# Low parts of seven weight tiles made by a ScalarE cast and an adding transfer instead of a VectorE subtraction

## The chip, the cores and the metric

The program runs on one core of one Trainium2 chip. The metric is the device time of one execution in microseconds (us), here the median of three runs. The profile is that of one further execution. Engines: PE is TensorE (PEld its weight loads), DVE is VectorE, ACT is ScalarE, POOL is GpSimd, SP is SyncE, which here only issues transfers.

## The reference, cut to what matters

Two transformer layers run over 256 context and 256 latent tokens of width 1024. The first layer mixes tokens by an mLSTM, the second by latent attention, and each is followed by a gated feed-forward with a convolution over time:

```python
def _conv_ffn(h, w_in, conv_w, conv_b, w_out):
    gate, up = jnp.split(h @ w_in, 2, axis=-1)
    return (jax.nn.silu(_dwconv(gate, conv_w, conv_b)) * up) @ w_out
...
x = _layer_norm(ALPHA * x + ml[2] * yl, ln_g[i, 0], ln_b[i, 0])
f = _conv_ffn(_modulate(x, ml[3], ml[4]), ffn_w_in[i], ffn_conv_w[i], ffn_conv_b[i], ffn_w_out[i])
x = _layer_norm(ALPHA * x + ml[5] * f, ln_g[i, 1], ln_b[i, 1])
```

The change is in the product `h @ w_in` of the second layer's feed-forward. There only the 256 latent tokens are left, and `w_in` is 1024 x 5632: 22 blocks of 128 columns of the gate and 22 of the up half.

## The kernel before, in words

**Products in two parts.** Every fp32 matrix is used as a sum of a rounded high part and a low part, both in the type fp32r, and a product is three matmuls: high by high, high by low, low by high. For weights the two parts are made on the fly by the class `Stream`. One tile is 128 x 1024 fp32 (512 KB). SP loads it into a raw buffer (`_load`, L308), ACT casts it to the high part h (`_split`, L345), and DVE writes the low part l = raw - h (`low`, L368). When the low part is made the raw buffer is given back (`self.raw.pop(j)`), and the next load may be issued into it. The order of all weight tiles is one list, made by `_plan`.

**Where the parts live.** A tile that is not `wide` takes one of NB = 3 buffers `w` that hold both parts. A `wide` tile takes two of the 31 general buffers `u` instead, which also hold activations, and is not counted against the three. `Stream.use(key)` hands out the next tile, and first calls `_split` for later tiles, up to AHEAD = 8 tiles past it, as long as the next one is wide or fewer than three `w` tiles are alive. From the attention output weights on, raw buffers are taken in a ring of nine: three of their own, three `u`, and three freed by other work.

**Order.** The program is written engine by engine as dataflow. A planner orders the instructions of each engine once, before the run, by the order of the program text and by its own estimate of when operands are ready, so an instruction may be put ahead of others that were written earlier. At run time each engine and each queue works through its list in order; waits are semaphores.

**The stage.** `aout_fin` ends the attention, normalizes, and starts the second feed-forward's input with its first five tiles: (`fin1`, p, j) for block p = 0, 1 and half j = 0, 1 (wide), and (2, 0). `ffn_in(1, ...)` takes the other 39 tiles in the order (2, 1), (3, 0), (3, 1), ... (21, 1). For one tile `both_mm` (L1503) issues 16 matmuls: eight of the high weights with 512 columns (the high and low parts of the 256 tokens side by side) and eight of the low weights with 256 columns, in the order seven high, eight low, one high. Then ACT copies half of the PSUM result (L1620) and DVE adds the halves (L1621). For each block the convolution, SiLU and gating follow (L728 to L735 on ACT and DVE, L1640), and the result is split into the tile `act` (L1648 ACT, L1649 DVE).

**Around it.** Through the first tiles of the stage a background generator, `ln_x`, finishes the residual: eight 512-column operations on DVE (L1518, L1520), each pair followed by a store that POOL issues (L1521, `x3d`). From about 1256 us on POOL issues the loads of the last normalization (L1566, L1215). After the stage, `outmm` multiplies the 22 `act` tiles by `w_out` (tiles `fout1`, matmul lines L430, L433, L434, results `y`), and `ln_rows` (L1229 on) ends the program on DVE and ACT.

Transfers that add to their destination exist already: for eight tiles of an earlier product, SP loads a first matrix, then POOL issues a transfer that adds a second one from device memory (L306), into a raw buffer of plain fp32. None of the kernel's transfers of that kind has its source in on-chip memory.

Of the kernel before, what the change touches and what calls it, by code (L numbers as in the profile page):

```python
# [11 lines left out]
ALU = mybir.AluOpType  # L12
# [58 lines left out]

YTAIL = 3


def _stat(w, m, kt0, nkt):
    k = w.shape[0] // 128
    a = w.reshape(k, 128, w.shape[1])[kt0:kt0 + nkt, :, m * 128:(m + 1) * 128]
    return a.transpose(1, 0, 2).reshape(128, nkt * 128)
# [7 lines left out]
def _plan():  # L86
    ids, order = {}, []

    def add(key, cols, wide=False):
        if key not in ids:  # L90
            ids[key] = (len(ids), cols)
        order.append((key, wide))

    for m in range(NUP, 16):
        add(("up", m, 0), 1024)
    for s in range(4):
        for c in range(4):
            add(("og", s, c), 1024)
    for p in range(2):

        for j in range(4):
            for n in ("vt2", "v11", "vt3", "vt1"):
                add((n, p, j), 1024)
        for j in range(4):
            for n in ("v21", "vt4", "v22"):
                add((n, p, j), 1024)
    for h in range(H0):
        for j in range(4):
            for c in range(2):
                add(("qk", (h * 2 + j) if j < 2 else (8 + h * 2 + j - 2), c), 1024)  # L110
    for g in range(2):
        for k in range(16):
            add(("mout", 0, k), 1024, k in MWIDE if g == 0 else k >= 16 - WIDE["mout"])
    for p in range(NF):
        add(("fin0", p, 0), 1024)
        add(("fin0", p, 1), 1024)
    cols = [1024] * 5 + [512]
    for j in range(6):
        for n in ("yt2", "y11", "yt3", "yt1"):
            add((n, 0, j), cols[j])  # L120
    for n in ("y21", "y22", "yt4"):
        for j in range(6):
            if (n, j) == ("yt4", 6 - YTAIL):
                for c, m in enumerate((3, 3, 2)):
                    add(("dkv", 0, c), m * 320)
            add((n, 0, j), cols[j], n == "yt4" and j >= 6 - YTAIL)
    for c in range(2):
        add(("ukn", 0, c), 1024, True)
    for c in range(2):
        add(("uv", 0, c), 1024, True)  # L130
    for c in range(4):
        add(("dq", 0, c), 768)
    for c, n in enumerate((2, 1)):
        add(("uqr", 0, c), n * 512)
    for c in range(3):
        add(("uqn", 0, c), 1024)
    for k in range(8):
        add(("aout", 0, k), 1024, k >= 8 - WIDE["aout"])
    for p in range(NF):
        add(("fin1", p, 0), 1024, p < 2)  # L140
        add(("fin1", p, 1), 1024, p < 2)
    for k in range(NF):
        add(("fout1", 0, k), 1024, k >= NF - WIDE["fout1"])
    return ids, order


def _pack(i):
    ids, _ = _plan()
    ws = np.zeros((len(ids), 128, CW), np.float32)
    gz = np.concatenate([i["m_w_gates"][0, 0], i["m_w_gates"][0, 1]], axis=1)  # L150
# [107 lines left out]
class Stream:  # L258
# [105 lines left out]
        return self.k.pool.tile([128, CW], F32R, tag="u", name="wu", bufs=NU)  # L364

    def low(self, j, src, h, l):
        n = src.shape[1]
        i = self.k.nc.vector.tensor_sub(l[:, :n], src, h[:, :n])  # L368
        self.k.behind(i, self.behind)
        self.made = i  # L370
        if self.order[j][0] == ("y21", 0, 1):
            self.second = i
        self.raw.pop(j)
        while self._room():
            self._load()
        return i
# [24 lines left out]
class K:  # L401
# [933 lines left out]
    def aout_fin(self, o1, pl, xr, gate, fi, h1u, att):  # L1335
# [21 lines left out]
        st.later = []  # L1357
        st.pump(fi + 4)
        low, st.later = st.later, None
        st.behind = lastw  # L1360
        st.pump(fi + 5)
# [570 lines left out]
    def ukn(self, g, heads=range(H1), held=None):  # L1932

        cs = slice(g * 256, (g + 1) * 256)
        for h in heads:
            w = self.wk[h // 4]
            if h % 2 == 0:
                ps = self.ps("kn")
            hs = slice((h % 2) * 256, (h % 2 + 1) * 256)
            for k in range(2):  # L1940
                c = slice((h % 4) * 256 + k * 128, (h % 4) * 256 + (k + 1) * 128)
                self.mm3(ps[:, hs], (w[0][:, c], w[1][:, c]), (self.ckT[k][:, 0, cs], self.ckT[k][:, 1, cs]),
                         k == 0, k == 1)
            if h % 2:
                lows = []
                for j in range(2):
                    hi, lo, src = self.kn[h - 1 + j][:, 0, cs], self.kn[h - 1 + j][:, 1, cs], ps[:, j * 256:(j + 1) * 256]
                    i = self.nc.scalar.copy(hi, src)
                    if held is not None:
                        self.tc.keep_in_program_order(i)  # L1950
                    lows.append(lambda lo=lo, src=src, hi=hi: self.nc.vector.tensor_sub(lo, src, hi))
                if held is not None:
                    held += lows
                else:
                    for low in lows:
                        low()
# [225 lines left out]
def build(tc, off, a, out):  # L2182
    es = ExitStack()
    with es:
        k = K(tc, es, off, a)
        nc = k.nc
        ids, order = _plan()
        k.st = st = Stream(k, ids, order, a["ws"])
        k.setup()
# [117 lines left out]
        for low in held:  # L2307
            k.behind(low(), k.normed)
# [54 lines left out]
```

## Time and profile before

| | |
|---|---|
| Runs | 1347.71, 1347.18, 1347.31 us; median 1347.31 |
| Profiled execution | span 1345.3 us from first to last instruction; 2.0 us less than the median of the runs, which also hold what lies before and after the span |
| Granted TensorE clock | 0.998 mean over the span, 1.00 in the changed stage |
| Busy share | PE 99%, PEld 83%, DVE 79%, ACT 53%, POOL 11% |
| Second feed-forward's input | matmuls from 1151.9 to 1276.3 us; the 39 tiles of `ffn_in` from 1167.35 us |
| Second feed-forward's output | 1276.3 to 1337.5 us, then 7.7 us of normalization and store |

Busy shares are means over the whole span; what an edit in one stage can move is read from that stage's rows. In a timeline row the first number is the start in us after the span's first instruction, the second the duration in us; brackets give the engine's idle time just before the row and what ended it.

### The profile page before, as it was taken

The numbers are of one execution on the slowest core, as the hardware profiler recorded it, in microseconds if no ns is written. First come the engines' busy times: TensorE is split into PE (matmuls) and PEld (weight loads), VectorE is DVE, ScalarE is ACT, GpSimd is POOL, SyncE is SP. The second block draws the span as 40 slices with busy tenths as digits, with TensorE's granted clock in tenths as the row PEclk, the third lists the DMA queues.
The fourth block names the chain that finished last, engine by engine and source line by source line (L and its number), as shares of the span: only waits on it lengthen the run. The fifth ranks groups of instructions, "written<-read, shape, count | busy, mean of one in ns | idle before, by whom it ended". The sixth has DMA issues, their size and how long they took to land.

```text
span 1345.3 us, 18750 instructions
## 1 busy us (share of the span) xinstructions
PE 1334.9 (99%) x6659; PEld 1120.2 (83%) x6659; DVE 1059.0 (79%) x1745; ACT 711.7 (53%) x1252; POOL 141.5 (11%) x236
## 2 busy tenths in 40 slices
PE   9999999999999999999999999999999999999997
PEld 5777888888888888888898888888888998988886
DVE  4798656678688696897979977758899889898874
ACT  4765444445744546474644334333566767676660
POOL 0222000011101011020002011111000002000100
PEclk9999999999999999999999999999999999999999
DMA  9988848889686384776628989967866437376750
GB/s 364 330 277 279 281 163 248 233 272 307 235 281 230 102 255 149 228 292 222 215 86 261 328 260 286 282 181 184 300 223 194 157 104 219 127 212 189 263 189 32
DMA packets 99885, 304.02 MB, mean 226 GB/s; under 512 B 12312, under 2 KB 25112, under 8 KB 99712
## 3 DMA queue, kind: packets, MB, share of 16 engines
q1 hardware_dynamic: 62992, 218.65, 48.6%
q0 software_dynamic: 26000, 66.75, 17.9%
q10 hardware_dynamic: 10800, 17.44, 3.6%
q8 instruction: 52, 0.85, 0.3%
q14 instruction: 41, 0.34, 0.1%
HBM read 272.21 MB, written 42.12 MB: 234 GB/s over the span
## 4 chain that ended last, share of the span: by engine, by line
PE 97%; DMA 1%; DVE 1%; ACT 0%; issue 0%; SPq 0%; DVEq 0%; ACTq 0%
PE fin L1503 8%; PE tok L430 6%; PE tok L434 6%; PE tok L433 6%; PE fin L433 6%; PE fin L434 6%; PE y L433 6%; PE fin L430 6%; PE y L434 6%; PE y L430 6%; PE qk L430 4%; PE qk L433 4%; PE qk L434 4%; PE up L718 2%; PE up L430 2%; PE up L434 1%
## 5 line engine op out<-in xcount | busy, mean ns | idle before, releaser
L368 DVE TENSOR_TENSOR w<-raw,w 128x1024 fp32r<-128x1024 f32 (+2 forms) x286 | 343.2, 1203 | 131.9 <-ACT w L345 129.7
L345 ACT CAST w<-raw 128x1024 fp32r<-128x1024 f32 (+2 forms) x286 | 296.2, 1037 | 282.4 <-PE tok L434 77.8
L544 DVE SCALAR_TENSOR_TENSOR junk<-ar,bc 128x1024 f32<-128x1024 f32 x128 | 156.1, 1219 | 5.2 <-ACT bc L586 2.3
L433 PE MATMUL fin<-h,w 128*128 128x512 f32 (+1 forms) x370 | 139.6, 377 | 0.0
L430 PE MATMUL fin<-h,w 128*128 128x512 f32 (+1 forms) x370 | 139.5, 377 | 0.0
L434 PE MATMUL fin<-h,w 128*128 128x512 f32 (+1 forms) x370 | 139.3, 377 | 0.0
L1503 PE MATMUL fin<-h,w 128*128 128x512 f32 (+1 forms) x636 | 111.1, 337 | 0.0
L1503 PEld LDWEIGHTS fin<-h,w 128*128 128x128 f32 x636 | 97.6, 190 | 13.2
L430 PE MATMUL qk<-xc,w 128*128 128x512 f32 x256 | 100.2, 391 | 0.0
L434 PE MATMUL qk<-xc,w 128*128 128x512 f32 x256 | 99.8, 390 | 0.0
L433 PE MATMUL qk<-xc,w 128*128 128x512 f32 x256 | 99.6, 389 | 0.0
L433 PEld LDWEIGHTS fin<-h,w 128*128 128x128 f32 x370 | 69.6, 188 | 13.0
L430 PEld LDWEIGHTS fin<-h,w 128*128 128x128 f32 x370 | 69.6, 188 | 12.9
L434 PEld LDWEIGHTS fin<-h,w 128*128 128x128 f32 x370 | 69.6, 188 | 12.6
L434 PEld LDWEIGHTS qk<-xc,w 128*128 128x128 f32 x256 | 48.0, 188 | 10.1
L430 PEld LDWEIGHTS qk<-xc,w 128*128 128x128 f32 x256 | 48.1, 188 | 9.8
L433 PEld LDWEIGHTS qk<-xc,w 128*128 128x128 f32 x256 | 48.1, 188 | 9.8
L430 PE MATMUL tok<-w,hT 128*128 128x512 f32 x128 | 49.9, 390 | 0.0
L433 PE MATMUL tok<-w,hT 128*128 128x512 f32 x128 | 49.8, 389 | 0.0
L434 PE MATMUL tok<-w,hT 128*128 128x512 f32 x128 | 49.8, 389 | 0.0
L735 ACT ACTIVATE fg<-fg 128x512 f32<-128x512 f32 (+1 forms) x44 | 23.1, 525 | 50.0 <-DVE fg L733 43.9
L368 DVE TENSOR_TENSOR wu<-raw,wu 128x1024 fp32r<-128x1024 f32 (+1 forms) x37 | 43.8, 1203 | 3.5 <-ACT wu L345 3.2
(486 smaller groups left out, 3125.7 us busy)
## 6 DMA issues: line engine op xcount, KB each, us to landing
raw<-in_ws SPq DMA_DIRECT2D x282, 512.0 KB, 4.5
ar<-in_adaT SPq DMA_DIRECT2D x80, 512.0 KB, 6.0
t4d<-in_ws POOLq DMA_DIRECT2D x20, 512.0 KB, 9.1
adaw<-in_ada SPq DMA_DIRECT2D x16, 512.0 KB, 8.0
zr<-fd ACTq DMA_DIRECT2D x33, 128.0 KB, 4.6
xmd<-xr POOLq DMA_DIRECT2D x16, 256.0 KB, 4.4
xcd<-cv POOLq DMA_DIRECT2D x16, 256.0 KB, 4.9
xs<-xmd POOLq DMA_DIRECT2D x16, 256.0 KB, 6.0
```

What stands on the lines that cost most here:

```text
L345: self.cast = k.nc.scalar.copy(h[:, :cols], src)
L368: i = self.k.nc.vector.tensor_sub(l[:, :n], src, h[:, :n])
L430: q = mm(out, w[0], x[0], start=start, stop=False, skip_group_check=on)
L433: mm(out, w[0], x[1], start=False, stop=False, skip_group_check=on)
L434: mm(out, w[1], x[0], start=False, stop=stop, skip_group_check=on)
L544: nc.vector.scalar_tensor_tensor(o, w, 1.0, self.bc[j], op0=ALU.mult, op1=ALU.mult, accum_out=col[:, k, j:j + 1])
L718: nc.tensor.matmul(ps[m], wk[i][:, c], hT[k][:, j], start=made[m] == 0, stop=made[m] == 23)
L735: nc.scalar.activation(tmp[:, :n], tmp[:, :n], AF.Silu)
L1503: self.nc.tensor.matmul(ps[:, 0:256] if x else ps, w[x][:, k * 128:(k + 1) * 128], h[:, 0:256] if x else h, start=i == 0 and not k0, stop= ...
```

## The change

Seven tiles, the up half (j = 1) of blocks p = 4 to 10, become wide: `_plan` marks them so, and their high and low parts go to two `u` buffers. Their low part is no longer written by DVE. ACT writes l = -raw, rounded to fp32r (the negative of h), and then POOL issues a transfer that adds the raw tile to l, from raw buffer to l buffer, both on chip. The raw buffer is free again when that transfer has landed. All other tiles keep the subtraction on DVE.

```diff
+DLOW = range(4, 11)
...
         add(("fin1", p, 0), 1024, p < 2)
-        add(("fin1", p, 1), 1024, p < 2)
+        add(("fin1", p, 1), 1024, p < 2 or p in DLOW)
...
     def low(self, j, src, h, l):
-        n = src.shape[1]
-        i = self.k.nc.vector.tensor_sub(l[:, :n], src, h[:, :n])
+        n, key = src.shape[1], self.order[j][0]
+        if key[0] == "fin1" and key[1] in DLOW and key[2]:
+            self.k.nc.scalar.mul(l, src, -1.0)
+            i = self.k.nc.gpsimd.dma_start(l, src, accum_op=ALU.add)
+        else:
+            i = self.k.nc.vector.tensor_sub(l[:, :n], src, h[:, :n])
```

## The prediction, made before the change was run

> **What bounds the kernel now.** I read the busy shares first, then the stage in windows, then the matmul row of that stage, because a share of 99% does not yet say whether the matmuls follow each other at their own pace.
>
> ```profile
> PE 1334.9 (99%) x6659; PEld 1120.2 (83%) x6659; DVE 1059.0 (79%) x1745; ACT 711.7 (53%) x1252; POOL 141.5 (11%) x236
> ...
> 1170.00:1200.00 30.00, 30.00 (x172) 26.32 (x171) 28.47 (x54) 22.27 (x43) 1.63 (x3) 1.00 0.62 195
> 1200.00:1260.00 60.00, 60.00 (x347) 52.84 (x346) 51.69 (x86) 40.84 (x77) 1.09 (x2) 1.00 0.65 193
> 1260.00:1280.00 20.00, 20.00 (x115) 17.53 (x114) 17.23 (x29) 14.25 (x26) 4.30 (x8) 1.00 0.92 315
> 1280.00:1320.00 40.00, 40.00 (x216) 34.59 (x215) 22.81 (x20) 19.91 (x21) 0.00 (x0) 1.00 0.44 145
> ```
>
> The columns of a window are its length, then busy time and count of PE, PEld, DVE, ACT and POOL, the granted clock, the busy share of the DMA engines and GB/s. From 1170 to 1320 us PE is busy throughout at clock 1.00. DVE is nearly full only from 1170 to 1200 (28.47 of 30 us); after that it has 8.3 us free in 60. The DMA engines stand at 0.62 to 0.65.
>
> ```profile
> 1167.35 109.10 PE L1503 MATMUL fin<-h,w 128*128 128x512 f32 x624
> 1276.28 0.40 PE L430 MATMUL y<-w,act 128*128 128x512 f32 x1
> 1220.62 0.37 ACT L1620 COPY fs<-fin 128x256 f32<-128x256 f32 x1 [1.17 <-PE fin L1503]
> 1226.20 0.37 ACT L1620 COPY fs<-fin 128x256 f32<-128x256 f32 x1 [1.17 <-PE fin L1503]
> ```
>
> The 624 matmuls are the 39 tiles of the stage, 16 each. They start at 1167.35 and the next stage's first matmul at 1276.28: 108.93 us, 2.793 us a tile. In the undisturbed middle the copy that waits for PE comes every 5.58 us for two tiles, 2.79 us a tile. So all 39 tiles together lose about 39 x 0.003 = 0.1 us to waits. PE is the bound here by its own pace, and a faster low part has 0.1 us to win.
>
> **What is removed.** Seven DVE subtractions.
>
> ```profile
> L368 DVE TENSOR_TENSOR w<-raw,w 128x1024 fp32r<-128x1024 f32 x42 | 51.3, 1223 | 6.3 <-ACT w L345 6.2
> L345 ACT CAST w<-raw 128x1024 fp32r<-128x1024 f32 x41 | 42.9, 1047 | 5.7 <-PE fin L1503 5.4 <-PE y L434 0.3
> L728 ACT ACTIVATE fg<-fs,sm 128x256 f32<-128x256 f32 x22 | 13.2, 600 | 0.5 <-DVE fs L1621 0.4
> L1620 ACT COPY fs<-fin 128x256 f32<-128x256 f32 x44 | 16.3, 370 | 26.9 <-PE fin L1503 25.8 <-PE fin L1489 0.9
> ```
>
> These groups are cut to 1160 to 1280 us. Seven times 1.223 is 8.6 us off DVE. None of it was on the path: worth 0, at most the 0.1 us above.
>
> **What is added on ACT.** Seven multiplications of 128 x 1024. The trace has none of that form; nearest is the cast of the same size, 1.047 us, which I take: 7.3 us. As an upper end, an activation with per-partition operands on 256 columns takes 0.600 against 0.370 for a copy, 0.23 more, so 1.28 us each, 9.0 us; fewer than the seven copies cannot be had, so the lower end is 7.3. ACT is free for 7.7 of the 30 us to 1200 and 19.2 of the next 60. The pressure is in the first 30: four tiles' multiplications (4.2 us) and about three casts that move forward (3.1 us) are 7.3 of 7.7 us. [...] Cost 0.
>
> **What moves: the run-ahead.** Wide tiles do not count against the three `w` buffers, so with every second tile wide, `use` splits five to seven tiles ahead instead of two. Tiles before the seven, and those well after them, keep their old lead. The first wide tile, (4, 1), is cast without waiting for PE to free a `w` buffer. Before, it did wait:
>
> ```profile
> 1163.71 1.05 ACT L345 CAST w<-raw 128x1024 fp32r<-128x1024 f32 x1 [4.54 <-PE fin L1503]
> 1170.95 1.05 ACT L345 CAST w<-raw 128x1024 fp32r<-128x1024 f32 x1
> 1173.14 1.05 ACT L345 CAST w<-raw 128x1024 fp32r<-128x1024 f32 x1 [0.84 <-PE fin L1503]
> 1178.53 1.21 DVE L368 TENSOR_TENSOR w<-raw,w 128x1024 fp32r<-128x1024 f32 x1
> 1181.96 0.37 ACT L1620 COPY fs<-fin 128x256 f32<-128x256 f32 x1 [0.25 <-PE fin L1503]
> ```
>
> The casts are those of tiles (3, 1), (4, 0) and (4, 1) in turn: counting the tiles of `ffn_in` from (2, 1) at 1167.35, the third `w` buffer comes free once per tile. The cast at 1173.14 was released by PE and not by its load, so its raw data lay ready. ACT stood idle for 4.54 us up to 1163.71; the planner puts later work into such holes, for it put the casts of (2, 1) and (3, 0) ahead of a normalization step that is written earlier:
>
> ```profile
> 1139.57 2.01 ACT L345 CAST w<-raw 128x1024 fp32r<-128x1024 f32 x2
> 1143.83 0.29 ACT L1380 ACTIVATE rs<-mv,keps 128x1 f32<-128x1 f32 x1 [2.26 <-DVE mv L1379]
> ```
>
> **What is added on POOL and the DMA engines.** Seven issues and seven 0.5 MB transfers that add. The nearest rows are the eight adding loads from device memory, and POOL's stores in this stage.
>
> ```profile
> L306 POOL DMA_DIRECT2D raw<-in_ws x8: 850/870/903, 218.6 to 324.7; - x8
> ...
> DMA to landing us min/median/max: 6.9/8.6/9.9
> 1168.90 0.55 POOL L1521 DMA_DIRECT2D x3d<-z  x1 [37.13 <-DVE z L1520]
> 1176.09 0.54 POOL L1521 DMA_DIRECT2D x3d<-z  x1 [3.18 <-ACT act L1648]
> 1256.58 0.55 POOL L1566 DMA_DIRECT2D xres<-x3d  x1 [79.94 <-ACT fg L735]
> ```
>
> An issue is 0.55 to 0.87 us, seven are 3.9 to 6.1 us on a POOL that idles from 1176.6 to 1256.6 us. From issue to landing I take 6.9 to 9.9 us, median 8.6. POOL works in order: an adding transfer that waits for ACT holds up the stores of `x3d` written behind it, and these are read back only after 1256 us, so 80 us cover them. The other way round, a store that waits for DVE (the last at 1176.09) holds up an adding transfer behind it; that is in the second case below.
>
> **When the first low part is needed.** PE finished tile (4, 1) just before the copy at 1181.96. Eight low matmuls and the last high one stand at its end; at 2.79 us a tile, the low ones are 0.12 us and the high ones 0.23, so 1.2 us: needed at 1180.8. Best case: cast and multiplication fill the hole before 1163.71, from 1159.2 to 1161.3; issued there, the transfer lands at 1168 to 1171, ten us early. Worst case: cast not before 1173.14, multiplied by 1175.2, landed at 1182.1 to 1185.1, and if queued behind the last store (1176.6) at 1183.5 to 1186.5: 1.3 to 5.7 us late. I take the early case as the likelier, since a raw tile in place, 4.54 idle us and free `u` buffers are what the planner needs. Later wide tiles have five or more tiles of 2.79 us between cast and use, 14 us, against 1.05 + 0.87 + 9.9 = 11.8 us: on time.
>
> [...]
>
> **Waits on PE.**
>
> ```profile
> L1503 PEldq EVENT_SEMAPHORE  x36: 51/51/51, 1172.6 to 1270.4; - x36
> ```
>
> The low weights now wait for a transfer and no longer for DVE. One more wait instruction per tile is 7 x 0.051 = 0.4 us if nothing hides it; the 36 there already, 1.8 us, cost at most the 0.1 us above, so 0.
>
> **Raw buffers and loads.** A raw buffer is now held until the transfer has landed, about 9 us longer for every second tile, and SP's list is in order behind it.
>
> ```profile
> SPq L308 <- DVE fg L1640: 34.6, 11, 3.5
> SPq L308 <- DVE act L1649: 22.0, 10, 2.2
> SPq L308 <- DVE w L368: 2.0, 1, 2.0
> L308 SPq DMA_DIRECT2D raw<-in_ws x54: 327/328/328, 1160.7 to 1301.5; - x54
> ...
> DMA to landing us min/median/max: 3.3/4.0/5.9
> ```
>
> From 1200 to 1260 SP waits 58.6 of 60 us for a buffer, and a load lands in 4.0 us; loads are held by buffers, not by bandwidth. Nine buffers turn once in 9 x 2.79 = 25.1 us. A plain tile needs 4.0 + 1.05 + 1.22 = 6.3 us of it, one of the seven 4.0 + 1.05 + 1.05 + 0.87 + 8.6 = 15.6: on average 14 us to spare. Cost 0.
>
> **Sum.** 0 removed from the path, 0 added: span 1345.3 and, with the 2.0 us around it, the median of 1347.3 again. Its own range is 1346.8 to 1348.0 (0.1 us gain, 0.4 us of waits, and the spread of the runs).
>
> **The rivals.** (A) *The first low part is late*, slower. Place: PE at the low matmuls of (4, 1). It decides if the adding transfer lands after 1180.8. For it: casts of that stretch ran late, POOL's last store issues at 1176.09, and no row tells whether the planner's estimate of an on-chip adding transfer holds. Against: the idle hole and the raw tile in place. Price 1.3 to 5.7 us, middle 3.5: 1350.8; not repeated, since each wait gives the next tile that much more time.
>
> (B) *The DMA engines fill up*, slower.
>
> ```profile
> q0 software_dynamic: 26000, 66.75, 17.9%
> ```
>
> The columns are packets, MB and the share of 16 engines' span: 17.9% of 1345.3 us for 66.75 MB is 3.6 us of all 16 engines per MB, 1.9 us per tile, or 3.8 if reading the destination too counts double. On 5.58 us that adds 0.34 to 0.68 to a share of 0.65: 0.99 to 1.33. Over 7 x 5.58 = 39 us the backlog is 0 to 12.9 us, and landings grow from 4.0 to 9.9. That is 18.8 against 14 to spare: up to 4.8 us, 1352.1. [...] No row here shows the on-chip kind.
>
> (C) *DVE's relief speeds PE up*, faster. Against it stand the 0.1 us above; the output stage behind is as dense. It would take 2.7 us, and there is no such idle time: 1347.2 at best by these rows.
>
> **How the numbers follow.** About 0.2% (2.7 us) is what a measurement of this kernel can tell from no change. No change 0.72 for the sum, and of A (0.16) and B (0.08) a small part, 0.04 together, stays within 2.7 us; ACT falling so far behind that PE waits, 0.02, slower; C 0.02, faster. That makes faster 0.02, same 0.76, slower 0.22. The range goes from 1346.3, one us under, to A's upper end, 1347.3 + 5.7 = 1353.0.
>
> **What the changed profile would show.** If right: the 624 matmuls again in about 109 us, 8.6 us less of L368's group, seven more ACT instructions of about 1.05 us, seven POOL issues, the first early, and no PE idle time. A shows as matmul idle time or stretched spacing near 1180 us ended by a transfer; B as a DMA share near 1.0 from 1175 to 1215 and casts that wait for loads; C as a shorter stage. I am wrong if ACT's or SP's order changes so that plain tiles come late, or if the adding transfer takes well over 10 us.

## The result, and the profile after

The changed kernel takes 1355.31 us (median of four runs, 1354.63 to 1356.99) against 1347.40 us for the kernel before beside it: a ratio of 1.0061, 95% interval 1.0049 to 1.0073. It is slower by 7.9 us; the forecast was no change, 1347.3, with 1353.0 as its upper end. The profiled execution has a span of 1354.2 us against 1345.3, 8.9 us more.

The lines of the change moved by a few: the cast L345 is now L347, VectorE's low part L368 is L374, the `fin` matmuls L1503 are L1509, the cast of `act` L1648 is L1654. New are the multiplication L371 on ACT and the adding transfer L372 on POOL.

First the busy shares, and the windows of the stage with the columns as before (length, then PE, PEld, DVE, ACT, POOL, granted clock, DMA share, GB/s).

```profile
PE 1339.2 (99%) x6659; PEld 1122.3 (83%) x6659; DVE 1051.9 (78%) x1738; ACT 718.4 (53%) x1259; POOL 147.5 (11%) x243
...
1170.00:1180.00 10.00, 8.90 (x50) 7.23 (x48) 9.57 (x20) 7.55 (x16) 1.62 (x3) 1.00 0.39 138
1180.00:1190.00 10.00, 7.64 (x24) 5.91 (x24) 5.04 (x10) 9.30 (x12) 2.60 (x3) 0.66 0.87 233
1190.00:1200.00 10.00, 8.34 (x47) 7.07 (x48) 4.54 (x10) 4.50 (x10) 0.85 (x1) 1.00 1.05 254
1200.00:1260.00 60.00, 60.00 (x347) 52.90 (x346) 46.73 (x84) 42.32 (x78) 2.54 (x3) 1.00 0.73 221
```

The loss lies between 1170 and 1200 us and nowhere else: from 1200 on PE is busy throughout, with the low parts of five of the seven changed tiles still to come. Two things happen in the bad stretch. PE's busy time falls short of 30 us by 5.1 us, and from 1180 to 1190 the granted clock is 0.66: PE counts as busy for 7.64 us there, yet shows only 24 matmuls in 10 us, where the 60 us after 1200 hold 58 in every 10. The waits of PE say for whom it stood:

```profile
PE fin L1509 <- ACT wu L347: 2.7, 1, 2.7
PE fin L1509 <- DMA wu<-raw: 2.0, 2, 1.6
PE fin L1509 <- DVE w L374: 0.4, 1, 0.4
```

The columns are the total, the count and the longest, in us. The largest wait is not for a transfer at all but for ACT's cast of the high part of (4, 1). The timeline around it (start, duration; in brackets the idle time before and what ended it):

```profile
1163.66 1.05 ACT L347 CAST w<-raw 128x1024 fp32r<-128x1024 f32 x1 [4.55 <-PE fin L1509]
...
1177.89 1.44 PE L1509 MATMUL fin<-h,w 128*128 128x256 f32 x9 [0.43 <-DVE w L374]
...
1179.64 1.05 ACT L347 CAST w<-raw 128x1024 fp32r<-128x1024 f32 x1
1180.59 0.41 ACT L1654 CAST act<-fg 128x256 fp32r<-128x256 f32 x1
1180.89 1.04 ACT L347 CAST wu<-raw 128x1024 fp32r<-128x1024 f32 x1
1181.84 1.06 ACT L371 ACTIVATE wu<-raw 128x1024 fp32r<-128x1024 f32 x1
1181.99 3.35 PE L1509 MATMUL fin<-h,wu 128*128 128x512 f32 x7 [2.65 <-ACT wu L347]
...
1185.14 4.26 PE L1509 MATMUL fin<-h,w 128*128 128x512 f32 x16
...
1189.24 0.40 PE L1509 MATMUL fin<-h,wu 128*128 128x512 f32 x1
1191.20 2.83 PE L1509 MATMUL fin<-h,wu 128*128 128x256 f32 x15 [1.57 <-DMA wu<-raw]
1194.49 1.44 PE L1509 MATMUL fin<-h,wu 128*128 128x256 f32 x9 [0.46 <-DMA wu<-raw]
1195.77 2.96 PE L1509 MATMUL fin<-h,w 128*128 128x512 f32 x16
1198.56 1.77 PE L1509 MATMUL fin<-h,wu 128*128 128x512 f32 x7
```

Four things are to be seen. ACT still has its 4.55 us hole before 1163.66: nothing was moved into it. The cast of (4, 1) stands at 1180.89, right behind a cast of `act`; ACT did the narrow cast of a much later tile (1179.64) first, although the raw tile of (4, 1) had been there since 1145.4 us by its load's record. After the 2.65 us of idle time the same seven matmuls that take 1.77 us at 1198.56 take 3.35 us, and the next sixteen 4.26 us instead of 2.96: TensorE runs at half pace, 512 columns every 0.427 us instead of 0.228. And the two transfer waits come after that.

The planner also ordered the matmuls of this stretch anew, as their starts show. Before, the fourteen matmuls of 512 columns from 1175.50 us held six high ones of (4, 1), ahead of the low ones of (4, 0) at 1178.70. With the high part of (4, 1) late these six no longer stand there, and PE stood 0.43 us for DVE's low part of (4, 0), which ends at 1177.84 us and ended at 1177.89 before. And between the seven high matmuls of (4, 1) and its eight low ones now stand all sixteen of (5, 0) and one of (5, 1), so its low part is needed seventeen matmuls later than in the kernel before.

Adding up what each start of a matmul is late against its usual spacing gives the loss: the wait for the low part of (4, 0) 0.70, the wait for the cast 2.82, the half pace 2.85, the two waits for transfers 1.84 and 0.72. Together that is 8.93 us, all of what the 624 matmuls take longer (from 1167.30 to 1285.16 us after, 108.93 before). The half pace alone cost a third of it.

The added instructions themselves cost what was expected:

```profile
L371 ACT ACTIVATE wu<-raw 128x1024 fp32r<-128x1024 f32 x7 | 7.4, 1052 | 0.0
...
L372 POOL DMA_DIRECT2D wu<-raw x7: 847/849/882, 1183.2 to 1211.0; - x7
...
DMA to landing us min/median/max: 7.9/8.6/11.7
```

### The profile page after: what moved, and what is told of

Its sections match the earlier page's. It is cut to its first block, busy times and chain, and to the rows that moved or that the text cites. A ratio compares the mean times of both kernels' runs of the same rounds, so it can differ in the third digit from the quotient of the medians.

```text
span 1354.2 us, 18775 instructions
## 1 busy us (share of the span) xinstructions
PE 1339.2 (99%) x6659; PEld 1122.3 (83%) x6659; DVE 1051.9 (78%) x1738; ACT 718.4 (53%) x1259; POOL 147.5 (11%) x243
## 4 chain that ended last, share of the span: by engine, by line
PE 97%; DMA 1%; DVE 1%; ACT 1%; issue 0%; SPq 0%; DVEq 0%
PE fin L1509 7%; PE y L439 6%; PE y L436 6%; PE y L440 6%; PE tok L436 6%; PE tok L440 6%; PE tok L439 6%; PE fin L439 6%; PE fin L440 6%; PE fin L436 6%; PE qk L436 4%; PE qk L439 4%; PE qk L440 4%; PE up L724 2%; PE up L436 1%; PE up L440 1%
## 5 line engine op out<-in xcount | busy, mean ns | idle before, releaser
L374 DVE TENSOR_TENSOR w<-raw,w 128x1024 fp32r<-128x1024 f32 (+2 forms) x279 | 334.5, 1202 | 130.1 <-ACT w L347 128.1
L347 ACT CAST w<-raw 128x1024 fp32r<-128x1024 f32 (+2 forms) x279 | 288.9, 1037 | 275.2 <-PE tok L440 74.0
L439 PE MATMUL fin<-h,w 128*128 128x512 f32 (+1 forms) x370 | 139.6, 377 | 0.0
L436 PE MATMUL fin<-h,w 128*128 128x512 f32 (+1 forms) x370 | 139.5, 377 | 0.0
L440 PE MATMUL fin<-h,w 128*128 128x512 f32 (+1 forms) x370 | 139.3, 377 | 0.0
L1509 PE MATMUL fin<-h,w 128*128 128x512 f32 (+1 forms) x524 | 94.3, 340 | 0.4 <-DVE w L374 0.4
L1509 PEld LDWEIGHTS fin<-h,w 128*128 128x128 f32 x524 | 81.9, 192 | 12.1 <-DVE w L374 0.9
L439 PEld LDWEIGHTS fin<-h,w 128*128 128x128 f32 x370 | 69.6, 188 | 13.0
L436 PEld LDWEIGHTS fin<-h,w 128*128 128x128 f32 x370 | 69.6, 188 | 12.8
L440 PEld LDWEIGHTS fin<-h,w 128*128 128x128 f32 x370 | 69.6, 188 | 12.6
L440 PEld LDWEIGHTS qk<-xc,w 128*128 128x128 f32 x256 | 48.1, 188 | 10.1
L347 ACT CAST wu<-raw 128x1024 fp32r<-128x1024 f32 (+1 forms) x44 | 44.8, 1043 | 8.0 <-DMA raw<-in_ws 7.9
```

The costliest lines, as they stand in the source:

```text
L347: self.cast = k.nc.scalar.copy(h[:, :cols], src)
L436: q = mm(out, w[0], x[0], start=start, stop=False, skip_group_check=on)
L439: mm(out, w[0], x[1], start=False, stop=False, skip_group_check=on)
L440: mm(out, w[1], x[0], start=False, stop=stop, skip_group_check=on)
L1509: self.nc.tensor.matmul(ps[:, 0:256] if x else ps, w[x][:, k * 128:(k + 1) * 128], h[:, 0:256] if x else h, start=i == 0 and not k0, stop= ...
```

## The experiments

The kernel before was run beside each of them, at 1347.16 to 1347.45 us. The theory at the start: the loss is one late start of the first wide tile, because the `u` buffers are handed out in the order of the program and (4, 1) gets its buffer only behind `act` tiles, and the adding transfer makes that later still. The rival: the loss is paid for each of the seven transfers, or by full DMA engines.

### The placement alone: wide tiles, VectorE's subtraction

```diff
-            self.k.nc.scalar.mul(l, src, -1.0)
-            i = self.k.nc.gpsimd.dma_start(l, src, accum_op=ALU.add)
+            i = self.k.nc.vector.tensor_sub(l[:, :n], src, h[:, :n])
```

> The seven tiles are wide as in the changed kernel, but their low parts are made by DVE as before; no adding transfer. Theory 1 (the buffers of one kind are given out in program order, so the cast of tile (4, 1) stands on ACT behind the third act tile and comes 7 us late): PE again waits about 2.7 us for that cast near 1179 to 1182, some 14 matmuls after it run at half pace (2.8 us), and the two waits for transfers (2.4 us) are gone: 1352.5 to 1354.5. Theory 2 (only the adding transfer's landing is late): no wait is left, 1346.5 to 1348.5.

Measured: 1352.61 us (1352.04 to 1354.02), ratio 1.0040 [1.0026, 1.0054]. The larger of the two waits of its PE in the stage (the other is again 0.4 us for DVE):

```profile
PE fin L1508 <- ACT wu L347: 2.7, 1, 2.7
```

With no adding transfer in the program, the wait for ACT is the same 2.7 us and the half pace follows it (10 matmuls of 512 and 8 of 256 columns at double spacing, from 1182.3 to 1188.4 us). So 5.4 of the 7.9 us come from where the tiles are placed, and not from the way the low part is made.

### The transfer alone: adding transfers, tiles stay in the `w` buffers

```diff
-        add(("fin1", p, 1), 1024, p < 2 or p in DLOW)
+        add(("fin1", p, 1), 1024, p < 2)
```

> The seven low parts come from ACT and the adding transfer, but the tiles stay in the three w buffers, two tiles ahead of PE. A low part can then be there no sooner than 1.05 (cast) + 1.05 + 0.87 + 8 = 11 us after PE frees the buffer, and PE needs it 2 x 2.79 + 1.6 = 7.2 us after that. Theory 1: the cast is on time, but each of the seven tiles waits 3 to 4 us for the transfer, with half-pace matmuls behind each wait: 20 to 45 us, 1368 to 1392. If the transfer's latency did not matter (theory 1 taken alone): 1347 to 1349.

Measured: 1357.71 us (1356.54 to 1358.97), ratio 1.0078 [1.0063, 1.0093].

```profile
PE fin L1509 <- DMA w<-raw: 8.7, 6, 2.2
```

With a lead of two tiles the transfer is late at each tile, as expected, but by 0.2 to 2.4 us, not by more: the size of the expectation was wrong by a factor of two or more. The expectation took 8 us from issue to landing; the seven transfers landed after 4.8 to 8.3 us. PE fell to half pace only once, after the last wait.

### One tile instead of seven, and seven later tiles

```diff
-DLOW = range(4, 11)
+DLOW = range(4, 5)      # one tile
+DLOW = range(12, 19)    # seven tiles in the quiet stretch
```

> The change on one tile alone, (4, 1). Theory 1 (the loss is one late start, not seven costs): PE waits 2.7 us for the late cast of (4, 1), then runs at half pace for some 6 us (2.8 us lost), then waits 1.5 to 2 us for its transfer: 1353 to 1355, nearly the whole loss of the change. Theory 2 (each of the seven tiles pays for its transfer): a seventh of 8 us, 1348 to 1349.

Measured: 1354.14 us (1353.13 to 1354.71), ratio 1.0050 [1.0033, 1.0066]. One tile costs 6.9 us, seven cost 7.9: it is one late start and not seven costs. Its waits of PE:

```profile
PE fin L1509 <- ACT wu L347: 2.7, 1, 2.7
...
PE fin L1509 <- DMA wu<-raw: 1.3, 1, 1.3
```

> The same change on the up half of blocks 12 to 18, where DVE and ACT have no backlog and no residual is finished beside it. Theory 1: the first wide tile is again cast only behind an act tile, close to its need, and its low part, 11 us after the cast, is late once: a wait of 3 to 6 us plus up to 3 us at half pace, 1351 to 1356. Rival (the loss comes from the crowded stretch 1170 to 1200, where ACT and DVE are behind): no loss, 1346.5 to 1348.5.

Measured: 1350.96 us (1350.79 to 1352.02), ratio 1.0031 [1.0020, 1.0042]. In the timeline of its PE the first wide tile is late here too, by its transfer, and a half-paced tile follows (sixteen matmuls in 4.29 us instead of 2.96):

```profile
1226.24 1.74 PE L1509 MATMUL fin<-h,wu 128*128 128x256 f32 x9 [1.97 <-DMA wu<-raw]
1227.77 4.29 PE L1509 MATMUL fin<-h,w 128*128 128x512 f32 x16
1231.90 2.96 PE L1509 MATMUL fin<-h,wu 128*128 128x512 f32 x16
```

The crowd of other work near 1180 us is therefore not needed for a loss; the first wide tile of a row is late in a quiet stretch too.

### The buffers given out early

If the order in which `u` buffers are given out is the cause, wide tiles that own their buffers from the start must be on time. A one-element memset on POOL, written at the end of `aout_fin`, takes them:

```diff
+        st.early = {("fin1", p, 1): (st.unit(), st.unit()) for p in DLOW}
+        for us in st.early.values():
+            for u in us:
+                nc.gpsimd.memset(u[0:1, 0:1].bitcast(F32), 0.0)
...
-            h, l = self.unit(), None
+            h, l = self.early.pop(key, None) or (self.unit(), None)
```

> As the changed kernel, but the 14 u buffers of the seven tiles are given out before the first act tile, by a one-element write of POOL into each (14 small instructions). Theory 1: the casts and multiplications of the first wide tiles go into ACT's idle time before 1163 us, the transfers land ten us before they are needed, and no PE wait is left: 1346.5 to 1349. Theory 2 (latency of the transfer): the waits for transfers stay, at least 2.4 us, with the half pace 5 or more: 1350 to 1354. Rival B of the prediction (DMA engines full): also above 1350.

Measured: 1356.77 us (1356.16 to 1357.31), ratio 1.0071: wrong. The first casts did go into the hole, at 1159 to 1167 us, and no wait for a transfer was left; but PE got another one:

```profile
PE fin L1514 <- ACT w L348: 6.6, 1, 6.6
```

ACT, which works in order, stood 7.55 us (to 1176.00) at the fourth wide tile's cast, whose load had not landed, and the cast of the plain tile (4, 0), next for PE, waited behind it until 1181.58. That load was not issued late (at 1164.63 us, against 1164.41 before) but landed after 11.3 us, at a DMA share of 0.93 from 1160 to 1180. DVE stood still too, 9.60 us up to 1176.16, for a transfer of another kind (the next run shows it), and ACT waited for DVE twice before it came to (4, 0). Which of the two stops would have been enough is not told apart. The fourteen buffers were taken for too many, and the next runs gave out those of the first three tiles and of the first two.

> As the changed kernel, with the u buffers of the first three of the seven tiles given out before the first act tile; the fourth and later ones follow the act tiles as in the changed kernel, so that no cast stands on ACT ahead of its load (which cost 7.5 us in the run with all 14 buffers early). Theory 1: casts of the first three by 1167, no wait of PE for ACT, at most one short wait for a transfer: 1346.8 to 1349.5. Theory 3 (the adding transfers beside the loads fill the DMA engines and delay the loads, whatever the order on ACT): PE waits again for a cast whose load is late, above 1351.

Measured: 1356.20 us (1355.15 to 1356.79), ratio 1.0066 [1.0051, 1.0081]: wrong again. Its waits of PE and the rows of POOL and DVE:

```profile
PE fin L1514 <- DVE w L375: 4.7, 1, 4.7
PE fin L1514 <- ACT w L348: 2.5, 1, 2.5
```

```profile
1148.99 0.81 POOL L1504 MEMSET wu<- 1x1 f32 x6 [32.52 <-PE y L1353]
1160.42 0.89 POOL L373 DMA_DIRECT2D wu<-raw  x1 [10.63 <-ACT wu L372]
1162.32 0.86 POOL L373 DMA_DIRECT2D wu<-raw  x1 [1.00 <-ACT wu L372]
1163.12 1.19 POOL L1222 DMA_DIRECT2D gr<-in_ln_g  x2
1164.22 1.15 POOL L1222 DMA_DIRECT2D br<-in_ln_b  x2
...
1174.58 0.69 DVE L1529 TENSOR_TENSOR z<-z,gr 128x512 f32<-128x512 f32 x1 [9.18 <-DMA gr<-in_ln_g]
```

The transfers are early now. But the broadcasts of the normalization's rows (`gr`, `br`), which before were issued by 1131 us, stand behind the memsets and two adding transfers on POOL and are issued at 1163 to 1165. They took 11 to 14 us to land, DVE waited 9.18 us for the first, and the low parts of plain tiles stood behind that on DVE. Two readings were left: POOL's order, or DMA engines too full for anything to land (their share was 0.99 from 1160 to 1180).

> As the run before, with the buffers of the first two of the seven tiles given out early. Theory 1: no wait for the first two; the third is cast behind an act tile at about 1185, and its low part, 11 us later, is some 5 us late against 1191: 1350 to 1356. If the run-ahead after the first two is enough, 1346.8 to 1349.

Measured: 1355.48 us (1354.07 to 1358.94), ratio 1.0065 [1.0050, 1.0081]. The third tile, whose buffers were not given out early, was late as expected (3.3 us, the first row), but the same trouble with ACT's cast of a plain tile came too (the second). The broadcasts stood behind an adding transfer again, and DVE waited 5.07 us for the first:

```profile
PE fin L1514 <- DMA wu<-raw: 3.3, 1, 3.3
PE fin L1514 <- ACT w L348: 2.2, 1, 2.2
```

> The seven tiles wide, three of them with early buffers, low parts by DVE, no adding transfer. Theory 1: the only thing that wide tiles alone cost was the late cast, and it is gone: 1346.5 to 1348.5, against 1352.6 without the early buffers. If wide tiles cost something else (buffers, order of loads): above 1350.

This is the run with three early buffers, with VectorE's subtraction in place of multiplication and transfer. Measured: 1347.50 us (1347.34 to 1347.81), ratio 1.0002 [0.9993, 1.0011]. No wait of PE is left in the stage, and the three casts stand here:

```profile
1158.86 2.01 ACT L348 CAST wu<-raw 128x1024 fp32r<-128x1024 f32 x2
1164.47 1.04 ACT L348 CAST wu<-raw 128x1024 fp32r<-128x1024 f32 x1
```

Against the first experiment only the moment at which six buffers are given out was changed (by six memsets on POOL, 0.81 us together), and the whole 5.4 us are gone. The place in the order of the buffers is the cause of that part.

### Early buffers, adding transfers, and POOL's order mended

```diff
+        self.gb = [self.bcast(self.a[n][2:3, :], s) for n, s in (("ln_g", "gr"), ("ln_b", "br"))]
         st.early = {("fin1", p, 1): (st.unit(), st.unit()) for p in range(4, 7)}
...
+        if ln == 2:
+            g, b = self.gb
```

> As the run with three early buffers and adding transfers (1356.2 us), but the broadcasts of the normalization's rows (gr, br) are issued on POOL ahead of the memsets and so ahead of the adding transfers, near 1125 to 1132 us as in the kernel before, instead of 1163 to 1165. Theory 1 in its present form (the transfer costs where it stands ahead of other work on an in-order queue): DVE no longer waits 9 us for gr at z, the low parts and adds behind it come on time, the first three transfers land before 1180, 1186 and 1191, and the time is 1347.3 to 1349. Rival (the DMA engines are full whatever the order): loads still land after 8 us or more from 1160 to 1180, casts and low parts of plain tiles wait for them, PE waits 3 us or more and falls to half pace, 1351 to 1357. If the transfers that now stand behind two stores of x3d are late at (5, 1) or (6, 1), PE waits for wu<-raw, 1349 to 1354, and neither is told apart.

Measured: 1346.78 us (1346.12 to 1347.13) against 1347.18 of the kernel before, ratio 0.9997 [0.9987, 1.0006]. The rows of POOL, then the windows:

```profile
1130.47 0.54 POOL L1222 DMA_DIRECT2D br<-in_ln_b  x1 [4.28 <-PE PT L2138]
1149.76 0.81 POOL L1505 MEMSET wu<- 1x1 f32 x6 [18.75 <-PE y L1353]
1161.19 0.89 POOL L373 DMA_DIRECT2D wu<-raw  x1 [10.62 <-ACT wu L372]
```

```profile
1170.00:1180.00 10.00, 10.00 (x57) 8.70 (x56) 9.81 (x21) 8.92 (x19) 1.32 (x3) 1.00 1.03 302
1180.00:1190.00 10.00, 10.00 (x61) 8.87 (x60) 8.09 (x16) 8.37 (x16) 0.89 (x1) 1.00 0.96 329
1190.00:1200.00 10.00, 10.00 (x59) 8.79 (x58) 6.52 (x13) 9.12 (x16) 2.24 (x3) 1.00 1.06 272
```

All seven adding transfers are in place, the DMA engines stand at 0.96 to 1.06 for 30 us, and PE does not wait once. DMA engines this full cost nothing in this order; in the run with three early buffers what cost was who stood behind whom. (The edit also put two of the `x3d` stores ahead of the second and third transfer, so it shows that POOL's order as a whole was the cause, not which of its pairs mattered most.) And with VectorE relieved, the time is that of the kernel before: nothing was to be won.

### The half pace by itself

The kernel before, with the cast of one tile in the quiet stretch delayed by `M` more casts of the same data ahead of it, and nothing else changed; `M` is 4, 5 and 6, one run each, without repeats:

```diff
+        if key == ("fin1", 14, 1):
+            for _ in range(M):
+                k.nc.scalar.copy(h[:, :cols], src)
         self.cast = k.nc.scalar.copy(h[:, :cols], src)
```

> The kernel before, with one tile, (14, 1) in the quiet stretch, cast late on purpose: ACT writes the same high part four more times before the cast that counts. Worked out from the rows of before (cast 1.05 us, two tiles of 2.79 us between cast and use, about 1 us of other ACT work in between), PE goes idle about 1 us. Theory (it is the length of PE's idle time that brings the half pace, and 2.1 us or more were needed so far): no half pace, span 1345.3 plus 1 to 2 us. Rival (any late start of a tile brings it): 3 us more.

> The same with five more casts: PE idle about 2 us. Theory: at the edge, where idle times of 2.09 us (no) and 2.13 us (yes) stood on both sides: span plus 2 to 3 us without the half pace, plus 4 to 6 us with it. Rival (half pace comes from late transfers or from DVE's work, not from PE's idle time): no half pace, since no transfer and no DVE work is changed here.

> The same with six more casts: PE idle about 3 to 4 us. Theory: matmuls of 512 columns spaced 0.427 us for 3.4 to 7 us after it, which loses 1.6 to 3.2 us on top of the idle time: span plus 5 to 8 us, with no adding transfer in the kernel. Rival (half pace comes from late transfers or from DVE's work): matmuls at 0.228 us right after the idle time, span plus 3 to 4.5 us.

The wait of PE in the three runs, in that order, each followed by a window of 5 us from there on:

```profile
1235.61 9.61 PE L1506 MATMUL fin<-h,w 128*128 128x512 f32 x52 [0.81 <-ACT w L348]
...
1235.00:1240.00 5.00, 4.39 (x23) 3.77 (x24) 4.96 (x8) 4.69 (x9) 0.00 (x0) 1.00 0.40 125
```

```profile
1236.50 8.79 PE L1506 MATMUL fin<-h,w 128*128 128x512 f32 x38 [2.71 <-ACT w L348]
...
1236.00:1241.00 5.00, 4.50 (x17) 3.93 (x18) 4.03 (x6) 2.38 (x5) 0.00 (x0) 0.66 0.59 188
```

```profile
1239.68 5.53 PE L1506 MATMUL fin<-h,w 128*128 128x512 f32 x20 [3.96 <-ACT w L348]
...
1239.00:1244.00 5.00, 4.32 (x16) 3.70 (x17) 3.17 (x5) 2.14 (x4) 0.00 (x0) 0.66 0.72 210
```

After a wait of 0.81 us the granted clock stays at 1.00; after 2.71 and 3.96 us it is 0.66 over the next 5 us, with 17 and 16 matmuls in them instead of 23. Spacings of 0.427 us stand from 1237.3 to 1240.7 in the second run and from 1240.0 to 1243.4 in the third, 3.4 us each, and lose 1.5 to 1.6 us on top of the idle time. The spans are 1346.7, 1349.1 and 1352.2 us: 1.4, 3.8 and 6.9 above the kernel before. Taking out what came before the stage (it starts 0.3 us later, 0.7 earlier and 1.2 later than there), 1.1, 4.5 and 5.7 are left, and start by start the lateness comes to 1.1, 4.5 and 5.8. No transfer was changed and no work was added on DVE, so the half pace comes from PE's idle time.

## Why the prediction was wrong

**The bound and the price of the instructions: right.** PE had nothing to win: with the order mended and VectorE relieved of seven subtractions the time is 0.9997 of before. The multiplication took 1.052 us (1.047 taken from the cast), an issue 0.85 to 0.88 (0.55 to 0.87), and the transfers landed after 7.9 to 11.7 us with a median of 8.6 (6.9 to 9.9, median 8.6). The adding loads of the earlier product were a good row for it here. In the other runs such transfers took 4.8 to 16.3 us; that both medians are 8.6 is in part luck. ACT's added work was put at 0, and ACT falling so far behind that PE waits at 0.02: no run shows how far PE can run ahead of ACT's copy out of PSUM (L1626), and in the changed kernel no wait of PE was for that copy; its one wait for ACT, 2.7 us, was for a cast.

**The run-ahead: the step that failed.** The prediction took "the early case as the likelier, since a raw tile in place, 4.54 idle us and free `u` buffers are what the planner needs". Free buffers there were: in the run with three tiles' buffers early, POOL wrote into six of them by 1149.8 us. What the tile lacked was its turn. Five of the seven wide casts in the changed kernel stand directly behind a cast of `act`, which takes `u` buffers earlier in the program (the other two behind the wide tile before), and with three tiles' buffers given out before, the casts stood at 1158.86 to 1164.47 us and the loss of the placement was gone. No row of the profile before shows whose turn it is for a buffer; that premise needed its own price and got none. The worst case, "cast not before 1173.14", was that of a `w` buffer, and the cast of the `u` buffer came 7.75 us later.

**Rival A named the place and undersized the price.** PE did lose its time at (4, 1), and the waits were not repeated for long, as argued: after two transfer waits the five tiles from 1200 us on cost nothing. But the first thing late at (4, 1) was the high part, by 2.82 us, ahead of the low part for which 1180.8 was worked out; with it came the 0.70 us at (4, 0), the transfers then added 2.56, and the half pace 2.85. The time 1180.8 also took PE's old order for granted. The first transfer landed at 1191.2 us, 10.4 later, and cost only 1.84 because PE was late itself by then and seventeen other matmuls had been put before the need. An upper end of 5.7 us for one late low part could not hold that.

**The half pace: a term that was missing.** Each wait was priced at its own length. The runs with a late cast show that a wait of 2.7 us costs 4.5.

**Rival B: fallen as it was priced.** The share did go to 1.05 as worked out (0.99 to 1.33), but in the run with POOL's order mended it stays at 0.96 to 1.06 for 30 us and PE waits for nothing. In the changed kernel no wait of PE was for a load either. Where it does show is the run with all fourteen buffers early: one load, issued at its usual time, landed after 11.3 us and ACT stood 7.55 us for it. What that alone cost stays open.

**Queues in order: half seen.** The prediction looked for stores behind the adding transfers and covered them with 80 us. It did not need more for this change; but in all three runs that gave buffers out early and kept the adding transfers in POOL's old order, broadcasts of rows stood behind transfers on POOL and DVE waited 5.1 to 9.6 us for the first. Only for the run with three early was it shown, by mending the order, that this was the cause.

**Rival C:** nothing gained, as the 0.1 us said.

## What to carry to other kernels

When an edit moves a tile from one buffer pool to another, find who is given that pool's buffers before it: run-ahead is limited by the order in which buffers are given out, and an idle engine, a landed load and free buffers prove nothing. A slow producer (here some 11 us from cast to landing against 2.3 on VectorE) is harmless only with that lead from its first tile on. Price a stall of TensorE at more than its length where it is over 2 us (here 1.5 to 2.9 us more in the runs with five and six more casts and in the changed kernel, nothing after a gap of 3.46 us in the run with two tiles' buffers early), and when a transfer is moved earlier on an in-order queue, list what now stands behind it.

## What the runs showed of the hardware

**An idle time of 2 to 3 us can halve TensorE's pace.** Counted from the start at which the next matmul was due, gaps of 0.98, 1.74, 1.87 and 2.09 us were followed by the usual pace, gaps of 2.13, 2.33, 2.35, 2.70, 2.82, 2.87, 4.12, 4.86 and 6.72 by spacings of 0.427 instead of 0.228 us; yet one of 3.46 us, in the run with two tiles' buffers early, was not. So length alone does not decide. The clock that the traces record is 0.5 for 3.4, 6.8 or 10.2 us at a time in this stage: 3.4 us in the runs with five and six more casts, 6.8 in the changed kernel, 10.2 in the run with all fourteen buffers early. In the changed kernel it falls at 1181.13 us, inside the gap that lasts from 1179.17, when the next matmul was due, to 1181.99; so the half-clock stretch starts neither with the gap nor at its end. Two stretches of the changed kernel, and two over which the gap of 3.46 us lies in the run with two tiles' buffers early (the clock is the third number from the end):

```profile
1177.71:1181.13 3.42, 1.44 (x9) 1.13 (x9) 3.16 (x8) 2.67 (x6) 0.00 (x0) 1.00 0.54 171
1181.13:1184.54 3.41, 2.55 (x6) 2.07 (x7) 3.32 (x5) 3.41 (x4) 0.88 (x1) 0.50 0.73 171
...
1194.32:1197.73 3.41, 1.74 (x8) 1.12 (x6) 2.10 (x6) 3.41 (x8) 1.02 (x2) 1.00 0.89 222
1197.73:1201.14 3.41, 1.78 (x12) 1.65 (x13) 2.20 (x4) 3.41 (x7) 0.68 (x1) 1.00 1.06 211
```

In the changed kernel 3.42 us with 1.44 us of work on PE stood ahead of the clock of 0.50. The gap of 3.46 us was shared out over two stretches of 3.41 us with 1.74 and 1.78 us of work, and the clock stayed at 1.00. How little work in how long a stretch it takes was not shown.

**An adding transfer between on-chip buffers took 7.9 to 11.7 us for 512 KB** in the changed kernel, 8.3 to 12.3 in the run with POOL's order mended, 4.8 to 8.3 with the tiles in the `w` buffers, and 16 us where several were early in one stretch. Plain loads of the same size took a median of 10.1 us from issue to landing with three of them early (from 1160 to 1200 us), and 8.3 in the run with POOL's order mended, against 4.0 in this stage of the kernel before. These medians rest on the 3, 6 and 19 loads whose landing the traces give.
